# Second layer of a two-layer decoder trunk: weights' pieces in one line with conversions four places behind their loads, the sink's column copied by ScalarE, second values fetched piece by piece, output stores on SyncE

## The chip, the core and the metric

The kernel runs on one core of a Trainium2 chip. The metric is the device time of one execution in microseconds. A core has five engines with instruction queues of their own: TensorE (PE) multiplies matrices into PSUM; VectorE (DVE), ScalarE (ACT) and GpSimd (POOL) do elementwise work; SyncE (SP) here issues most of the DMAs. An engine works through its queue in order: an instruction that has to wait holds up all that stand behind it. ACT can issue DMAs as well.

## What is computed

```python
# layer 1: multi-scale retention; layer 2: sliding-window attention. Both: x + gated branch @ w_out
def swa_layer(x, g_norm, w_in, q_gain, k_gain, sinks, w_out, k_buf=None, v_buf=None):
    h = rmsnorm(x, g_norm)
    proj = h @ w_in
    q, k, v, gate = jnp.split(proj, [SWA_Q, SWA_Q + SWA_KV, SWA_Q + 2 * SWA_KV], axis=-1)
    q = rmsnorm(q.reshape(B, L, SWA_KV_HEADS, SWA_GROUP, SWA_HD), q_gain)
    k = rmsnorm(k.reshape(B, L, SWA_KV_HEADS, SWA_HD), k_gain)
    ...
    scores = jnp.einsum('bnqkgd,bnskd->bnkgqs', qb, kk) * (SWA_HD ** -0.5)
    scores = jnp.where(valid, scores - alibi_slopes() * dist, NEG)
    p = softmax(concatenate([scores, sink_col], -1))[..., :-1]
    o = jnp.einsum('bnkgqs,bnskd->bnqkgd', p, vv)
    ...
    o = o * jax.nn.silu(gate)
    return x + o @ w_out, new_k, new_v
```

There are 1024 prompt tokens in one sequence and 8 single tokens of decode batches with a cache of 128 keys and values each. The model width is 1024. Layer 2 has 16 query heads of 64 in two groups (g = 0, 1) that share a key and a value head, and a window of 128. All is float32; the kernel splits each matmul operand into a rounded high part and the rest, and does three matmuls per product (high x high, high x low, low x high).

## The kernel before, in words

The change lies in layer 2, whose steps are these.

**Weights.** A slot is a block of 1024 x 256 of a weight matrix, `wh` (high) and `wl` (low), three slots in a ring. It is filled in four pieces of 256 KB: SP loads `wr` (L1642, a ring of three), ACT rounds it to `wh` (L1648), POOL subtracts to get `wl` (L1649). There are twelve slots: four for queries, four for gates, four for the output matrix. `job()` is called at fixed places in the program; each call takes a step or a few of the foremost slot's list: three loads at once, nothing in the two calls that end with the marks, then the first conversion, the fourth load and the second conversion, then a conversion per call. `ready` runs the rest of a list at once if a product needs the slot.

**Keys and values** (`kv_mm`, `kv_ev`, `kv_vs`, `kv_v4`). Nine products, for 8 chunks of 128 tokens and the decode tokens, alternate between two PSUM pools, `pj` and `sc`. The values are stored to memory (`vscr2`) and fetched from there in another order as `V4` (L1824), four DMAs for each half; those of group 1 are fetched when group 0 is done, eight DMAs at one place.

**Attention.** A unit ("duo") is one chunk of 128 tokens with four heads (head pair pp = 0 to 3), 32 units in all, one to each step m of a loop that has four steps more at its end. In a step, PE does the scores (`att_s`, L2053), DVE adds the bias (`att_e`, L2069; before it a copy of the sink's column, L2065), takes the maximum (L2074), ACT does four exponentials (`att_p`, L2080), DVE a reciprocal, POOL the normalisation (L2085), DVE a transposition (L2090 and L2093). For the first chunk (c = 0) POOL fills a part of the scores with a constant (L2073) before the maximum. For odd pp PE multiplies with the values two steps later (`att_o`, L2111), and DVE applies the gate (`att_out`). Between these parts stand five calls `fill(src, W)`, which lay about 1 us of projection matmuls each (L1698 to L1700) into PE's queue: first the tiles of queries and gates, then those of the output. A tile goes into one of two `pj` buffers; ACT evicts queries (L1915, L1916), DVE and ACT gates (L1930, L1935, L1941). `decode(m, s)` puts the decode tokens' steps in between, by a table.

**Output** (`so_all`, `so_y`). 24 tiles (ft, ti) of 128 features and a token group ti: 384 tokens for ti = 0, 1 and 264 (256 and the 8 decode tokens) for ti = 2. For each: the residual is loaded (`xr`, L2321, for ti = 2 also L2323; two buffers), 24 matmuls, an add on DVE (L2334), a transposition on DVE (L2263) into `yo`, and four stores (L2266); for ti = 2, one tile later, a transposition on PE, an eviction on ACT (L2272) and a small store (L2273) as well. While attention runs, the four stores are issued by SP, after it by ACT. The small store is on ACT's queue throughout. The last two tiles go another way (L2281).

PE's order is the order of the program, which the scheduler does not alter; the same holds for the other engines in layer 2.

Of the kernel before, what the change touches and what calls it, by code (L numbers as in the profile page):

```python
# [67 lines left out]
def _trunk(ctx, tc, nc, a):  # L68
# [1559 lines left out]
    jobs = []  # L1628

    def wslot(src, turn=True):  # L1630

        slot, box = [], {}

        def first():
# [10 lines left out]
        def conv(i):  # L1645
            js = slice(2 * i, 2 * i + 2)
            raw = box[i]
            nc.scalar.activation(box["hi"][:, js, :], raw, AF.Copy)  # L1648
            nc.gpsimd.tensor_tensor(box["lo"][:, js, :], raw, box["hi"].bitcast(F32)[:, js, :], ALU.subtract)  # L1649
# [4 lines left out]
        slot.append(box)  # L1654
        return slot

    def steps_of(slot, n):
        todo = slot[-1]["todo"]
        for _ in range(n):
            x = todo.pop(0)  # L1660
            while x is None:
                x = todo.pop(0)
            x[0](*x[1:])

    def job():
        while jobs:
            if not jobs[0]["todo"]:
                jobs.pop(0)
                continue
            x = jobs[0]["todo"].pop(0)  # L1670
            if x is None:
                return
            x[0](*x[1:])
            if x[0].__name__ == "conv" and (not jobs[0]["todo"] or jobs[0]["todo"][0][0].__name__ == "conv"):
                return

    def ready(slot):
        box = slot[-1]
        while box["todo"]:
            job()  # L1680
        return slot

    soon = []
# [43 lines left out]
    def w_col(kind, pp):  # L1727
        return wslot(w_in_swa[:, (0 if kind == "q" else 1280) + 256 * pp:(0 if kind == "q" else 1280) + 256 * pp + 256])

    slots = {("q", 0): w_col("q", 0)}  # L1730
    steps_of(slots["q", 0], 4)
# [90 lines left out]
    def kv_v4(h, g=0):  # L1822
        for b in range(4):
            nc.sync.dma_start(out=V4[32 * b:32 * b + 32, 16 * h:16 * h + 16, :],  # L1824
                              in_=vscr2[512 * h:512 * h + 512, 64 * g:64 * g + 64].rearrange("(k i) f -> i k f", i=32))
# [82 lines left out]
    def group_proj(gr):  # L1908
# [16 lines left out]
        def g_ev(pp, pl, ti, ps):  # L1925
# [14 lines left out]
            def rest():  # L1940
                nc.vector.scalar_tensor_tensor(gt, gt, 1.0, gv, ALU.add, ALU.mult)  # L1941
                if ti == 2:
                    nc.vector.scalar_tensor_tensor(gd, gd, 1.0, gxd, ALU.add, ALU.mult)
                    nc.vector.tensor_scalar(gd, gd, 0.5, None, ALU.mult)
# [56 lines left out]
    def ms_ev(xy, pp, ti, sq):  # L2001
# [56 lines left out]

    def att_e(u, xy):
        pp, c = u.pp, u.c  # L2060
        rq = RQ[pp, u.ti]
        st = u.st = atp.tile([128, 4, 161], F32, name="s", bufs=2)
        mx = atp.tile([128, 4], F32, name="mx", bufs=3)
        sm = u.sm = atp.tile([128, 4], F32, name="sm", bufs=3)
        nc.vector.tensor_copy(st[:, :, 160], snk[:, 4 * pp:4 * pp + 4])  # L2065
# [34 lines left out]
    def att_o(u):  # L2100
# [12 lines left out]
        if u.c == 7 and u.g == 0:  # L2113
            later_v4.append(1)

    later_v4 = []
# [112 lines left out]
    def dec_out():  # L2229
        nc.vector.tensor_tensor(god, god, gdec2, ALU.mult)  # L2230
# [26 lines left out]
    def so_y(ft, ti, yt):  # L2257
# [3 lines left out]
        if (ft, ti) not in LAST:  # L2261
            yo = atp.tile([128, 384], F32, tag="qs", name="yo", bufs=6)
            nc.vector.transpose(yo[:, :npr], yt[:, :npr])  # L2263
            for q in range(4):
                f0 = ft * 128 + 32 * q
                (nc.sync if attn[0] else nc.scalar).dma_start(  # L2266
                    out=y_p[0, t0:t0 + npr, f0:f0 + 32].rearrange("(b r) c -> r b c", r=32),
                    in_=yo[32 * q:32 * q + 32, :npr].rearrange("r (b c) -> r b c", c=32))
            if ti == 2:
# [3 lines left out]
                nc.scalar.dma_start(out=y_s[:, 0, ft * 128:ft * 128 + 128], in_=yo[:8, 256:384])  # L2273
# [100 lines left out]
    for n in range(9):  # L2374
# [21 lines left out]
        if 1 <= n <= 4:  # L2396
            steps_of(slots["q", 0], 2 if n == 1 else 1)
        if n == 2:
            slots["q", 1] = w_col("q", 1)
            steps_of(slots["q", 1], 1)  # L2400
            slots["g", 0] = w_col("g", 0)
            steps_of(slots["g", 0], 1)
            jobs.pop()
            jobs.append(slots["q", 1][-1])
        if 2 <= n <= 4:
            steps_of(slots["g", 0], 1)
        if n == 7:
            kv_v4(0)
        if 5 <= n <= 8:
            steps_of(slots["g", 0], 2 if n == 5 else 1)  # L2410
# [11 lines left out]
    kv_v4(1)  # L2422
# [3 lines left out]
    fill(ps, 2.0)  # L2426
    pt = dec_cache(0)
    dec_cache_ev(0, pt)
    fill(ps, 2.0)
    pt = dec_cache(1)  # L2430
# [8 lines left out]
    pvp = xq_.enter_context(tc.tile_pool(name="pvp", bufs=1, space=PSUM))  # L2439
    fill(ps, 1.0)  # L2440
    xy = xy_tile()
    ms_ev(xy, *msq[0], ms_mm(xy, *msq.pop(0)))
    for _ in range(4):
        fill(ps, 1.08)
        now()
        job()
    now()
    left = [1]

    def both():  # L2450
# [10 lines left out]
             (33, 4): (dec_soft, 5), (34, 0): (dec_soft, 6), (34, 1): (dec_vload,), (34, 3): (dec_pt,), (35, 2): (dec_o,),  # L2461
             (35, 3): (dec_out,)}
# [6 lines left out]
    for m in range(NU + 4):  # L2469
# [26 lines left out]
        decode(m, 0)  # L2496
        for fn, args in pend_m:
# [16 lines left out]
        if later_v4:  # L2514
            later_v4.clear()
            kv_v4(0, 1)
            kv_v4(1, 1)
# [16 lines left out]
        x = u  # L2534
        fill(src, W)
    for b in jobs:
        while b["todo"]:
            job()
# [44 lines left out]
```

## Time and profile before

| | |
|---|---|
| three runs | 1262.64, 1262.62, 1257.4 us; median 1262.62 |
| profiled execution | 1262.77 us, span 1261.0 us |
| busy share of the span | PE 97%, DVE 60%, POOL 55%, ACT 47% |
| mean granted clock of PE | 0.993 |
| layer 2, from 905 to 1261 us | PE 328.85 of 356 us busy |

The page gives the busy time of each engine and the chain that ended last. For layer 2 the views that matter are the order in time of one engine, where a number in brackets is idle time of the engine before that instruction with what ended it; the stretches, which give busy time by engine and the granted clock of PE; and the waits of one engine, summed by what it waited for.

### The profile page before, as it was taken

To read this page: it belongs to the slowest core of one execution; us is meant where nothing else is said; L and a number is where in the kernel's file an instruction comes from. 1 tells how busy PE (TensorE), PEld (TensorE's weight loads), DVE (VectorE), ACT (ScalarE), POOL (GpSimd) and SP (SyncE) were. 2 spreads that over 40 slices of the span, in tenths; PEclk is the share of its full clock that TensorE was granted. 3 is DMA by queue.
4 is the path that set the end of the run, shared out by engine and by line. 5 is a ranking of instruction groups with operands and counts; after the bars stand their busy time and mean duration, and the time that the engine had idled before them with its cause. 6 is when DMAs were issued, how large, how long until landed. Compare 5 with 4: busy or idle time off the path is not lost. (4 is left out here: it accounts for less than half of the span.)

```text
span 1261.0 us, 29403 instructions
## 1 busy us (share of the span) xinstructions
PE 1220.8 (97%) x11304; PEld 1155.4 (92%) x11304; DVE 752.9 (60%) x1462; ACT 587.6 (47%) x1482; POOL 689.5 (55%) x740
## 2 busy tenths in 40 slices
PE   7999999999999999999999999999899997999998
PEld 6999999999999999978889999999889886998997
DVE  6954646665666665367775476675255774678421
ACT  6533445545455555478773234454444443454000
POOL 6654544525549899889773266744544453445010
PEclk9999999999999999999999999999989999999999
DMA  6313866677676875365788964774422355155354
GB/s 220 106 55 119 253 198 213 209 232 224 183 226 176 230 221 156 114 199 175 243 259 194 291 202 152 202 224 117 129 68 75 115 159 114 64 188 165 75 130 86
DMA packets 259882, 213.10 MB, mean 169 GB/s; under 512 B 72681, under 2 KB 230757, under 8 KB 259726
## 3 DMA queue, kind: packets, MB, share of 16 engines
q1 hardware_dynamic: 215376, 178.75, 48.4%
q10 hardware_dynamic: 44366, 32.47, 8.6%
q8 instruction: 89, 1.46, 0.5%
q14 instruction: 51, 0.42, 0.1%
HBM read 139.03 MB, written 73.17 MB: 168 GB/s over the span
## 5 line engine op out<-in xcount | busy, mean ns | idle before, releaser
L334 PE MATMUL b<-xh,woh 128*128 128x258 f32 x784 | 223.2, 285 | 0.0
L336 PE MATMUL b<-xh,wol 128*128 128x258 f32 x784 | 221.8, 283 | 0.3 <-POOL wol L225 0.3
L335 PE MATMUL b<-xl,woh 128*128 128x258 f32 x784 | 221.6, 283 | 0.0
L1698 PE MATMUL pj<-SA,wh 128*128 128x384 f32 (+1 forms) x576 | 192.3, 334 | 13.7 <-ACT qs L1916 9.8
L1700 PE MATMUL pj<-SA,wl 128*128 128x384 f32 (+1 forms) x576 | 186.2, 323 | 0.0
L1699 PE MATMUL pj<-SA,wh 128*128 128x384 f32 (+1 forms) x576 | 185.5, 322 | 0.0
L334 PEld LDWEIGHTS b<-xh,woh 128*128 128x128 f32 x784 | 148.0, 189 | 4.1 <-issue 4.1
L335 PEld LDWEIGHTS b<-xl,woh 128*128 128x128 f32 x784 | 148.7, 190 | 0.0
L336 PEld LDWEIGHTS b<-xh,wol 128*128 128x128 f32 x784 | 148.0, 189 | 0.5 <-POOL wol L225 0.5
L225 POOL TENSOR_TENSOR wol<-raw,woh 128x512 fp32r<-128x512 f32 x51 | 66.8, 1318 | 118.0 <-ACT woh L220 106.8
L1698 PEld LDWEIGHTS pj<-SA,wh 128*128 128x128 f32 x576 | 110.0, 191 | 23.2 <-ACT qs L1916 10.5
L327 PE MATMUL b<-woh,xh 128*128 128x256 f32 x448 | 126.6, 283 | 0.0
L328 PE MATMUL b<-wol,xh 128*128 128x256 f32 x448 | 126.0, 281 | 0.0
L329 PE MATMUL b<-woh,xl 128*128 128x256 f32 x448 | 125.6, 280 | 0.0
L1649 POOL TENSOR_TENSOR wl<-wr,wh 128x512 fp32r<-128x512 f32 x48 | 61.6, 1298 | 92.0 <-ACT wh L1648 88.6
L1699 PEld LDWEIGHTS pj<-SA,wh 128*128 128x128 f32 x576 | 110.4, 192 | 0.0
L1700 PEld LDWEIGHTS pj<-SA,wl 128*128 128x128 f32 x576 | 109.9, 191 | 0.0
L327 PEld LDWEIGHTS b<-woh,xh 128*128 128x128 f32 x448 | 84.3, 188 | 5.0 <-issue 2.9
L329 PEld LDWEIGHTS b<-woh,xl 128*128 128x128 f32 x448 | 84.3, 188 | 0.0
L328 PEld LDWEIGHTS b<-wol,xh 128*128 128x128 f32 x448 | 84.3, 188 | 0.0
L220 ACT ACTIVATE woh<-s 128x512 fp32r<-128x512 f32 x88 | 54.1, 623 | 60.1 <-POOL s L210 22.4
L225 DVE TENSOR_TENSOR wol<-s,woh 128x512 fp32r<-128x512 f32 x88 | 67.4, 769 | 20.0 <-ACT woh L220 19.7
(515 smaller groups left out, 3158.4 us busy)
## 6 DMA issues: line engine op xcount, KB each, us to landing
raw<-in_w_in_ret_dram ACTq DMA_DIRECT2D x44, 512.0 KB
st<-in_state_ret_dram SPq DMA_DIRECT2D x64, 256.0 KB
out_dram<-st SPq DMA_DIRECT2D x64, 256.0 KB
vb<-vscr SPq DMA_DIRECT2D x64, 128.0 KB
evp<-qks SPq DMA_DIRECT2D x32, 256.0 KB
evx<-vsc SPq DMA_DIRECT2D x32, 256.0 KB
wr<-in_w_in_swa_dram SPq DMA_DIRECT2D x32, 256.0 KB
pbs<-pb SPq DMA_DIRECT2D x16, 320.0 KB
```

Source lines behind the costliest of these rows:

```text
L220: act(s.op[name, sub][0], src_of(s, name, sub), AF.Copy)
L225: eng.tensor_tensor(lo, src_of(s, name, sub), hi.bitcast(F32), SUB)
L327: mm(dst, xh, wh, start=a and i == 0, stop=False, skip_group_check=True)
L328: mm(dst, xh, wl, start=False, stop=False, skip_group_check=True)
L329: mm(dst, xl, wh, start=False, stop=z, skip_group_check=True)
L334: mm(dst, wh, xh, start=a, stop=False, **sg)
L335: mm(dst, wh, xl, start=False, stop=False, **sg)
L336: mm(dst, wl, xh, start=False, stop=z, **sg)
L1649: nc.gpsimd.tensor_tensor(box["lo"][:, js, :], raw, box["hi"].bitcast(F32)[:, js, :], ALU.subtract)
L1698: mm(ps, hi[:, k, fs], xh[:, k, t0:t1], start=first and k == ks[0], stop=False)
L1699: mm(ps, hi[:, k, fs], xl[:, k, t0:t1], start=False, stop=False)
L1700: mm(ps, lo[:, k, fs], xh[:, k, t0:t1], start=False, stop=last and k == ks[-1])
```

## The change

The list of steps per slot becomes one line of pieces for all slots. At most three pieces are loaded and not yet converted. Each `job()` loads as many as that allows, and converts the oldest if it was loaded at least four calls ago; there is one more call in each step of the loop (five instead of four), and some in the stretch before it. `job` also issues one of the eight fetches of second values, which stand in a list. The sink's column is written by ACT (`att_k`), for the next unit at the end of a step. The factor 0.5 of the decode gate moves into a later product. The copy of `ms` goes from DVE to ACT. Keys and values swap their PSUM pools, so that the ninth product sits in `sc`. The first query slot's loads and conversions keep their places; the second query slot's loads stand ahead of the second value fetches. Three decode steps come one or two places later. The stores of `so_y` are always issued by SP, also the small one.

```diff
-        box["todo"] = [(first,), (load, 0), (load, 1), (load, 2), None, None, (conv, 0), (load, 3)] + [
-            (conv, i) for i in range(1, 4)]
-        jobs.append(box)
...
+    def job(lag=4):
+        tick[0] += 1
+        while pieces and len(flight) < 3:
+            box, i = pieces.pop(0)
+            if "hi" not in box:
+                box["alloc"]()
+            box["load"](i)
+            flight.append((box, i, tick[0]))
+        if flight and flight[0][2] <= tick[0] - lag:
+            box, i, _ = flight.pop(0)
+            box["conv"](i)
+        if later_v4:
+            kv_v4(*later_v4.pop(0))
...
-            kvst[c] = (pjp.tile([128, 512], F32, tag="pj", name="pj") if c % 2 == 0 else
+            kvst[c] = (pjp.tile([128, 512], F32, tag="pj", name="pj") if c % 2 else
...
-                    nc.vector.tensor_scalar(gd, gd, 0.5, None, ALU.mult)
...
-            nc.vector.tensor_copy(ms.rearrange("p (l j r) -> p l j r", l=2, j=2),
-                                  xy[0:1, :, 448:464].rearrange("p j (l r) -> p l j r", l=2))
+            nc.scalar.activation(ms.rearrange("p (l j r) -> p l j r", l=2, j=2),
+                                 xy[0:1, :, 448:464].rearrange("p j (l r) -> p l j r", l=2), AF.Copy)
...
+    def att_k(u):
+        u.st = atp.tile([128, 4, 161], F32, name="s", bufs=2)
+        nc.scalar.activation(u.st[:, :, 160], snk[:, 4 * u.pp:4 * u.pp + 4], AF.Copy)
...
-        nc.vector.tensor_copy(st[:, :, 160], snk[:, 4 * pp:4 * pp + 4])
...
-            later_v4.append(1)
+            later_v4.extend((b_, h, 1) for h in range(2) for b_ in range(4))
...
-        nc.vector.tensor_tensor(god, god, gdec2, ALU.mult)
+        nc.vector.scalar_tensor_tensor(god, god, 0.5, gdec2, ALU.mult, ALU.mult)
...
-                (nc.sync if attn[0] else nc.scalar).dma_start(
+                nc.sync.dma_start(
...
-                nc.scalar.dma_start(out=y_s[:, 0, ft * 128:ft * 128 + 128], in_=yo[:8, 256:384])
+                nc.sync.dma_start(out=y_s[:, 0, ft * 128:ft * 128 + 128], in_=yo[:8, 256:384])
...
-             (33, 4): (dec_soft, 5), (34, 0): (dec_soft, 6), (34, 1): (dec_vload,), (34, 3): (dec_pt,), (35, 2): (dec_o,),
-             (35, 3): (dec_out,)}
+             (33, 4): (dec_soft, 5), (34, 0): (dec_soft, 6), (34, 1): (dec_vload,), (35, 0): (dec_pt,), (35, 3): (dec_o,),
+             (35, 4): (dec_out,)}
...
         decode(m, 0)
+        job()
...
-        if later_v4:
-            later_v4.clear()
-            kv_v4(0, 1)
-            kv_v4(1, 1)
...
+        if m + 1 < NU:
+            att_k(duos[m + 1])
```

What this does to SP's queue is seen best at two places. The first is step m = 17, where group 0 is done. `V` are the value fetches, `wr` the weight loads, `pbs` and `oscr` stores that wait for DVE. SP's rows before:

```order
L2091 DMA pbs<-pb 128x640
L2141 DMA oscr_h<-oh 128x4x128
L2142 DMA oscr_l<-ol 128x4x128
L1824 DMA V_11385<-vscr_75 32x16x64 x8
L1642 DMA wr<-in_w_in_swa_dram 128x2x256 x3
L2010 DMA ms_11366<-ms 4x1x8
L1642 DMA wr<-in_w_in_swa_dram 128x2x256
```

And after:

```order
L1821 DMA V_11385<-vscr_75 32x16x64 x2
L2090 DMA pbs<-pb 128x640
L2138 DMA oscr_h<-oh 128x4x128
L2139 DMA oscr_l<-ol 128x4x128
L1821 DMA V_11385<-vscr_75 32x16x64
L1643 DMA wr<-in_w_in_swa_dram 128x2x256 x3
L1821 DMA V_11385<-vscr_75 32x16x64 x3
L2006 DMA ms_11366<-ms 4x1x8
L1821 DMA V_11385<-vscr_75 32x16x64
L2090 DMA pbs<-pb 128x640
```

The eight fetches no longer stand in one block ahead of the three loads; three stand ahead of them, and five behind.

The second place is the output, after the end of attention. `xr` are the residuals' loads, `yo` the stores. SP's rows before, from tile (1,1)'s load to tile (4,1)'s:

```order
L2321 DMA xr_15961<-xscr 128x384
L2321 DMA xr_16007<-xscr 128x384
L2321 DMA xr_16042<-xscr 128x384
L2321 DMA xr_16077<-xscr 128x256
L2323 DMA xr_16077<-xdec 128x8
L2321 DMA xr_16107<-xscr 128x256
L2323 DMA xr_16107<-xdec 128x8
L1642 DMA wr<-in_w_out_swa_dram 128x2x256 x3
L2321 DMA xr_16155<-xscr 128x384
```

And after, from tile (3,1)'s load to the small store of tile (1,2):

```order
L2318 DMA xr_16034<-xscr 128x384
L2263 DMA out_dram<-yo 32x12x32 x4
L2318 DMA xr_16069<-xscr 128x256
L2320 DMA xr_16069<-xdec 128x8
L2318 DMA xr_16099<-xscr 128x256
L2320 DMA xr_16099<-xdec 128x8
L1643 DMA wr<-in_w_out_swa_dram 128x2x256 x3
L2263 DMA out_dram<-yo 32x8x32 x4
L2270 DMA out_dram<-yo 8x128
L2318 DMA xr_16147<-xscr 128x384
L2263 DMA out_dram<-yo 32x8x32 x4
L2270 DMA out_dram<-yo 8x128
```

Before, only loads stood there; now each group of four stores, and the small stores, stand between the load of one tile and that of a later one.

More of the change, by code (lines that the diff above doesn't have):

```diff
@@ L1626, in _trunk, with wslot, alloc @@
     wp = ctx.enter_context(tc.tile_pool(name="wp", bufs=1, reuse_waits="tile"))
[L1628 to L1634, printed above, removed]
+    pieces, flight, tick = [], [], [0]
+    def wslot(src, turn=True, auto=True):
+        box = dict(n=0)
+        slot = [box]
+        def alloc():
             box["hi"] = wp.tile([128, 8, 256], F32R, tag="wh", bufs=3, name="wh")
@@ L1649, in conv @@
             nc.gpsimd.tensor_tensor(box["lo"][:, js, :], raw, box["hi"].bitcast(F32)[:, js, :], ALU.subtract)
-        box["todo"] = [(first,), (load, 0), (load, 1), (load, 2), None, None, (conv, 0), (load, 3)] + [
-            (conv, i) for i in range(1, 4)]
-        jobs.append(box)
-        slot.append(box)
-        return slot
[L1657 to L1675, printed above, removed]
+            box["n"] += 1
+        box.update(alloc=alloc, load=load, conv=conv)
+        if auto:
+            pieces.extend((box, i) for i in range(4))
+        return slot
+    def job(lag=4):
[11 more added lines that the diff above has]
+            kv_v4(*later_v4.pop(0))
     def ready(slot):
-        box = slot[-1]
-        while box["todo"]:
-            job()
+        while slot[-1]["n"] < 4:
+            job(0)
         return slot
-    soon = []
+    soon, later_v4 = [], []
     def now():
@@ L1725, in io, with w_col @@
         return iop2.tile([128, 384], dt, tag=tag, bufs=bufs, name=tag)
[L1727 to L1731, printed above, removed]
+    def w_col(kind, pp, auto=True):
+        c0 = (0 if kind == "q" else 1280) + 256 * pp
+        return wslot(w_in_swa[:, c0:c0 + 256], True, auto)
+    slots = {("q", 0): w_col("q", 0, False)}
+    wq0 = slots["q", 0][-1]
+    wq0["alloc"]()
+    for j in range(3):
+        wq0["load"](j)
     iop2 = ctx.enter_context(tc.tile_pool(name="iop2", bufs=1))
@@ L2061, in att_e @@
         rq = RQ[pp, u.ti]
[L2062 removed]
+        st = u.st
         mx = atp.tile([128, 4], F32, name="mx", bufs=3)
         sm = u.sm = atp.tile([128, 4], F32, name="sm", bufs=3)
[L2065 removed]
         for pl in range(2):
@@ L2396, in _trunk @@
         if 1 <= n <= 4:
-            steps_of(slots["q", 0], 2 if n == 1 else 1)
+            wq0["conv"](n - 1)
+        if n == 1:
+            wq0["load"](3)
         if n == 2:
[L2399 to L2404, printed above, removed]
+            slots["q", 1] = w_col("q", 1, False)
+            slots["q", 1][-1]["alloc"]()
+            slots["g", 0] = w_col("g", 0, False)
+            wg0 = slots["g", 0][-1]
+            wg0["alloc"]()
         if 2 <= n <= 4:
-            steps_of(slots["g", 0], 1)
+            wg0["load"](n - 2)
         if n == 7:
-            kv_v4(0)
+            for b in range(4):
+                kv_v4(b, 0, 0)
         if 5 <= n <= 8:
-            steps_of(slots["g", 0], 2 if n == 5 else 1)
+            wg0["conv"](n - 5)
+        if n == 5:
+            wg0["load"](3)
     sg_.close()
@@ L2421, in _trunk @@
     kv_tr(7)
-    kv_v4(1)
+    pieces.extend((slots["q", 1][-1], i) for i in range(4))
+    job()
+    for b in range(4):
+        kv_v4(b, 1, 0)
     kv_out()
@@ L2534, in _trunk @@
         x = u
+        if m + 1 < NU:
+            att_k(duos[m + 1])
         fill(src, W)
-    for b in jobs:
-        while b["todo"]:
-            job()
+    while pieces or flight:
+        job(0)
     xq_.close()
```

15 lines of the change are left out of this document (9 added, 6 removed).

## The prediction

> **What bounds the kernel now.** I read the page first, then the stretches of 20 us, the order in time of TensorE (PE) with its idle times, the waits of ScalarE (ACT), and last the chain that ended last.
>
> ```profile
> span 1261.0 us, 29403 instructions
> PE 1220.8 (97%) x11304; PEld 1155.4 (92%) x11304; DVE 752.9 (60%) x1462; ACT 587.6 (47%) x1482; POOL 689.5 (55%) x740
> ```
>
> The run took 1262.77 us, 1.8 more than its span and 0.15 above the median of 1262.62. PE is busy for 97% of it, so no part can give much except where PE stands idle or runs slowly. The change touches only layer 2, from about 860 us on. There the idle times of PE and the granted clock are few and easy to find:
>
> ```profile
> 900.00:920.00 20.00, 15.51 (x199) 13.95 (x188) 3.67 (x14) 8.42 (x21) 9.98 (x10) 0.86 0.22 79
> 920.00:940.00 20.00, 20.00 (x225) 18.98 (x232) 13.20 (x34) 8.12 (x27) 11.69 (x8) 0.97 0.28 87
> ...
> 1040.00:1060.00 20.00, 15.78 (x282) 14.96 (x283) 10.94 (x31) 8.39 (x29) 8.77 (x10) 0.91 0.42 90
> 1060.00:1080.00 20.00, 15.66 (x176) 13.56 (x175) 9.33 (x22) 9.30 (x33) 8.64 (x8) 0.91 0.45 116
> ...
> 1180.00:1200.00 20.00, 18.57 (x106) 17.54 (x104) 5.83 (x12) 1.04 (x5) 0.00 (x0) 0.91 0.43 96
> ```
>
> ```profile
> 915.24 0.59 PE L1698 MATMUL pj<-SA,wh 128*128 128x264 f32 x1 [4.49 <-ACT qs L1916]
> ...
> 983.37 1.09 PE L2111 MATMUL o<-R,V 32*64 32x128 f32 x40 [1.95 <-DVE R L2093]
> ...
> 1032.58 1.42 PE L2111 MATMUL o<-R,V 32*64 32x128 f32 x80 [0.97 <-issue]
> ...
> 1044.22 0.59 PE L1698 MATMUL pj<-SA,wh 128*128 128x264 f32 x1 [4.80 <-ACT qs L1916]
> ...
> 1069.94 0.44 PE L1698 MATMUL pj<-SA,wh 128*128 128x384 f32 x1 [3.62 <-DVE sq L1930]
> ...
> 1182.53 0.67 PE L104 MATMUL xy<-ident,rbc 16*128 16x16 f32 x9 [1.37 <-DVE rbc L2196]
> ```
>
> The second column of a stretch is PE's busy time, the third last the granted clock. Each long idle time costs twice: 4.49 us of waiting at 915, then (0.14 + 0.03) x 20 = 3.4 us of clock; 4.80 at 1044 and 3.62 at 1070, each with 0.09 x 20 = 1.8 us of clock. What they wait for is an ACT that stands still itself:
>
> ```profile
> ACT wh L1648 <- DMA wr<-in_w_in_swa_dram: 29.3, 11, 6.2
> ```
>
> In eleven places ACT waits in its conversion of a weight piece for that piece to land, 29.3 us in all, and the PSUM evictions behind it wait too. From 1160 us on something else ends last. The chain that ended last is a loop over output tiles, no longer PE:
>
> ```profile
> 1167.44 0.57 DVE sq L2334
> ...
> 1187.65 0.57 DVE sq L2334
> 1188.24 0.59 DVE yo L2263
> 1188.85 0.33 SPq L2266
> ...
> 1190.78 2.52 DMA xr<-xscr
> 1193.39 0.57 DVE sq L2334
> ...
> 1199.48 0.57 DVE sq L2334
> ```
>
> The residual is added to a tile (sq), VectorE (DVE) transposes it (yo), SyncE (SP) issues its four stores, and only then the load of the next tile's residual (xr), for which the next add waits. One turn takes 1193.39 - 1187.65 = 5.74 us; the five turns from 1167.44 to 1199.48 took 6.41 on average. PE runs two tiles ahead, all that its two buffers allow; at 1200 it has to wait for an add, so the lead is used up:
>
> ```profile
> 1200.10 0.44 PE L1698 MATMUL pj<-SA,wh 128*128 128x384 f32 x1 [0.16 <-DVE sq L2334]
> ```
>
> **The change part by part.**
>
> *Weights' pieces in one line.* A conversion now stands four places behind its load, in PE's program some 5 us instead of 2. The three long idle times, one by one. At 915 two things were late: ACT's conversions, and the memory fill of the first unit's scores on GpSimd (POOL), queued behind three conversions:
>
> ```profile
> 906.22 1.26 DVE L2069 SCALAR_TENSOR_TENSOR s<-xy,rq,ndp 128x160 f32<-128x160 f32 x4 [4.71 <-PE xy L2053]
> 907.01 3.79 POOL L1649 TENSOR_TENSOR wl<-wr,wh 128x512 fp32r<-128x512 f32 x3 [3.20 <-DMA wr<-in_w_in_swa_dram]
> 910.74 1.55 POOL L2073 MEMSET s<- 32x512 f32 x4
> 912.32 0.82 DVE L2074 TENSOR_REDUCE mx<-s 128x4 f32<-128x644 f32 x1 [4.84 <-POOL s L2073]
> ...
> 914.62 0.56 ACT L1916 ACTIVATE qs<-pj,gq 128x384 f32<-128x384 f32 x1
> ```
>
> The new order loads this slot ahead of the value fetches and cache copies and converts earlier, so the fill can start when DVE is done at 907.48. Then fill 1.55, maximum 0.82, and from its end to the eviction's end 915.18 - 913.14 = 2.04: done at 911.9. PE stood from 910.75, so 1.15 us of the wait stays, hidden by nothing. Saved: 3.3 us, and the 3.4 of clock if so short a wait brings none: 6.7. At 1044 the same fill (the unit is again the first of its head pair) keeps about as much: 4.80 - 1.15 + 1.8 = 5.4. At 1070 ACT waited for this:
>
> ```profile
> 1054.28 6.26 SPq L1824 DMA_DIRECT2D V<-vscr  x8
> ...
> 1065.80 1.26 ACT L1648 ACTIVATE wh<-wr 128x512 fp32r<-128x512 f32 x2 [6.20 <-DMA wr<-in_w_in_swa_dram]
> ```
>
> Eight fetches of second values held SP for 6.26 us ahead of the loads of the next slot. They are now issued one at each place and the loads after three of them; the fetched values are first used some eight units later. Saved: 3.62 + 1.8 = 5.4. The 1.95 at 983 has the same cause (DVE behind a tanh that stood behind a conversion) and goes; the 0.97 at 1032 goes with DVE's relief, below. Sum: 6.7 + 5.4 + 5.4 + 1.95 + 0.97 = 20.4. What is late next, wherever PE comes earlier, is the chain scores, maximum, exponentials, normalisation of each unit, and loads that stand behind SP's waits for DVE. I take 18 us; the ends are 10 (the third long wait goes whole, a third of the rest) and 24 (the two waits of 1.15 go too, and small ones not listed).
>
> *Sink's column on ACT, one product less on DVE.*
>
> ```profile
> L2065 DVE COPY s<-snk 128x4 f32<-128x4 f32 x32 | 11.2, 349 | 0.0
> ...
> L1944 DVE TENSOR_SCALAR gdec<-gdec 128x8 f32<-128x8 f32 x8 | 3.6, 448 | 0.3
> ```
>
> ```profile
> 1134.84 0.19 ACT L1938 ACTIVATE gdec<-sq 128x8 f32<-128x8 f32 x1
> ```
>
> DVE loses 14.8 us of busy time; PE waits for DVE in few places, all counted above. The nearest row for the copy on ACT is 0.19 us, so 32 of them take 6 us of an engine that is busy 47%. The copy waits for the buffer that DVE frees one unit earlier; behind it stand the next evictions, but ACT had to wait for that same DVE to get here. Nothing, with 1 us to each side.
>
> *Swap of PSUM pools for keys and values, later decode steps.* PE has no idle time in the key stage but one of a microsecond at its start, so plus or minus 1. The 1.37 at 1182 goes with the later step, but PE is ahead of the adds there: nothing.
>
> *Stores on SP.* With the stores on ACT, the last 16 adds went about at PE's pace. In the new order each load of a residual stands behind the stores of the tile before, to the end, so the turn of the chain applies to all of them. The rows that it needs:
>
> ```profile
> 1205.20 0.32 SPq L2321 DMA_DIRECT2D xr<-xscr  x1
> ...
> 1207.55 0.43 DVE L2334 TENSOR_TENSOR sq<-pj,xr 128x264 f32<-128x264 f32 x1 [1.76 <-DMA xr<-xdec]
> ...
> 1252.95 0.56 DVE L2334 TENSOR_TENSOR sq<-pj,xr 128x384 f32<-128x384 f32 x1 [2.94 <-PE pj L1700]
> 1255.88 0.43 DVE L2334 TENSOR_TENSOR sq<-pj,xr 128x264 f32<-128x264 f32 x1 [2.38 <-PE pj L1700]
> ```
>
> ```profile
> 1239.44 1.94 ACTq L2266 DMA_DIRECT2D out_dram<-yo  x4
> 1241.73 0.29 ACTq L2273 DMA_DIRECT2D out_dram<-yo  x1
> ```
>
> From add to load is 1190.78 - 1187.65 = 3.13 us; a load of 384 columns then takes 2.6 to its add, one of 264 takes 1207.55 - 1205.20 = 2.35. From the add of tile (1,1) at 1199.48 to the last, the new order has: two plain turns, 11.5; three that end in a narrow tile, 3.13 + 2.35 = 5.5 each, 16.4; four behind a narrow tile's stores (add and transposition 0.9, four stores 1.9, small store 0.3, load 2.35 or 2.6) 5.5 to 5.75 each, 22.5; three behind two tiles' stores (2 x 1.9 + 0.3 + load 2.6 + add and transposition 1.1), 7.8 each, 23.3; four adds whose load follows at once, 0.9 each, 3.5. Together 77.2. Before it was 1255.88 - 1199.48 = 56.4. The cost is 20.8 us. Its cover would be PE's lead, and that is spent by 1200. With 5.4 us in a quiet turn it is 17, with the 6.41 of the busy turns 29.
>
> **Sum:** 1262.8 - 18 + 20.8 = 1265.6 us.
>
> [...] A narrow tile's 24 matmuls take PE 1255.88 - 1252.95 = 2.9 us, a wide one's 384/264 of that, 4.3; so in turns of 5.5 to 5.8 us PE will wait 1.5 to 2.6. The row at 1182.53 shows that 1.37 us came with a stretch at 0.91. [...]
>
> **The rivals.** *The loop on SP stays hidden.* If residuals land in time after all, the tail goes at PE's pace, and the 1.71 us at
>
> ```profile
> 1232.67 0.27 PE L104 MATMUL tr<-ident,sq 128*8 128x128 f32 x1 [1.71 <-ACT yo L2272]
> ```
>
> go too, since ACT no longer stands in store issues: 1262.8 - 18 - 1.7 = 1243.1. For it speaks that two residual buffers exist; against it that SP's new order has no place where a load overtakes the stores, and that this loop is seen between 1167 and 1199. *The gains don't come.* If the fill on POOL and the loads behind SP's waits keep PE standing as long as a late conversion did, with 8 us gained, it is 1262.8 - 8 + 20.8 = 1275.6, slower; it decides from under 14.5 us of gain (1269). *The clock falls in the tail.*
>
> ```profile
> 1200.00:1261.00 61.00, 54.88 (x373) 53.84 (x373) 14.59 (x32) 5.31 (x14) 5.08 (x4) 0.98 0.51 105
> ```
>
> PE has 54.9 us of work there. If each of some twelve waits costs 1.8 us of clock, that is 76.5, still under 77.2; if 3.4, as at 915, it is 95.7 and PE is last again: 18.5 more, 1284.
>
> **How the numbers follow.** 0.5%, about 6.3 us, is what a measurement of this kernel can tell from no change: 1256.3 to 1268.9. Forecast 0.62, of which 0.44 falls within that, 0.13 above, 0.05 below. Loop hidden 0.12, faster. Gains missing 0.20, of which 0.04 within. Clock 0.06, slower. So faster 0.17, same 0.48, slower 0.35. The range, 1254 to 1279, takes in the ends of gain (24 with a cost of 17: 1255.8) and of cost (18 with 29: 1273.8; 8 with 24: 1278.8), and leaves out the hidden loop and the clock.
>
> **What would show it.** Right: ACT's waits for wr fall from 29.3 us to a few; no PE idle time over 2 us between 900 and 1150; the first add of an output tile comes about 18 us earlier; from then on every add waits for xr, at 5.5 to 6.4 us a turn and near 7.8 behind two tiles' stores, with PE idle in each. Wrong: adds in the tail that wait for PE (then 1243), a long PE wait still at the first unit of a head pair (then 1276), or a clock well under 0.9 after 1180.

## The result and the profile after

The changed kernel takes 1267.18 us (median, 1265.94 to 1270.85), the kernel before, beside it on the same chip, 1261.15 us (1257.4 to 1262.64). The ratio is 1.0055, with a 95% interval from 1.0034 to 1.0076: half a per cent more. The forecast was 1265.6 in a range from 1254 to 1279.

Behind the small difference stand two large ones. The first rows are the head of the page after; then come ACT's waits, then PE's order in time in layer 2, where the brackets hold the idle time ahead of an instruction and what ended it.

```profile
span 1264.1 us, 29412 instructions
PE 1223.8 (97%) x11304; PEld 1158.3 (92%) x11304; DVE 737.5 (58%) x1418; ACT 590.8 (47%) x1518; POOL 690.6 (55%) x740
```

```profile
ACT wh L1649 <- DMA wr<-in_w_in_swa_dram: 8.5, 5, 4.0
```

```profile
908.69 0.39 PE L1692 MATMUL pj<-SA,wh 128*128 128x264 f32 x1 [1.37 <-ACT qs L1913]
...
1028.29 0.39 PE L1692 MATMUL pj<-SA,wh 128*128 128x264 f32 x1 [2.10 <-ACT qs L1913]
...
1189.22 0.39 PE L1692 MATMUL pj<-SA,wh 128*128 128x264 f32 x1 [2.63 <-DVE sq L2331]
...
1210.35 0.59 PE L1692 MATMUL pj<-SA,wh 128*128 128x264 f32 x1 [3.71 <-DVE sq L2331]
...
1242.45 0.69 PE L1692 MATMUL pj<-SA,wh 128*128 128x384 f32 x1 [4.54 <-DVE sq L2331]
```

ACT's waits for weight pieces fell from 29.3 us to 8.5, and of PE's long waits before the output two short ones are left. In their place PE now waits in the output, for adds on DVE. What the adds wait for is seen in their own rows, from tile (1,1) to the end:

```profile
1177.05 0.56 DVE L2331 TENSOR_TENSOR sq<-pj,xr 128x384 f32<-128x384 f32 x1 [4.10 <-DMA xr<-xscr]
1182.78 0.56 DVE L2331 TENSOR_TENSOR sq<-pj,xr 128x384 f32<-128x384 f32 x1 [4.56 <-DMA xr<-xscr]
...
1201.88 0.56 DVE L2331 TENSOR_TENSOR sq<-pj,xr 128x384 f32<-128x384 f32 x1 [5.76 <-DMA xr<-xscr]
1209.74 0.56 DVE L2331 TENSOR_TENSOR sq<-pj,xr 128x384 f32<-128x384 f32 x1 [6.49 <-DMA xr<-xscr]
...
1234.11 0.56 DVE L2331 TENSOR_TENSOR sq<-pj,xr 128x384 f32<-128x384 f32 x1 [4.78 <-DMA xr<-xscr]
1241.84 0.56 DVE L2331 TENSOR_TENSOR sq<-pj,xr 128x384 f32<-128x384 f32 x1 [6.36 <-DMA xr<-xscr]
...
1249.39 0.56 DVE L2331 TENSOR_TENSOR sq<-pj,xr 128x384 f32<-128x384 f32 x1 [1.11 <-PE pj L1694]
1257.85 1.03 DVE L2331 TENSOR_TENSOR sq<-pj,xr 128x384 f32<-128x384 f32 x2 [7.08 <-DMA xr<-xscr]
```

`x2` in the last row stands for two adds, one right behind the other. All of the adds shown but one (at 1249.39) wait for the residual xr, from 1201.88 to 1241.84 for 4.8 to 6.5 us. A plain turn takes 5.73 us (1177.05 to 1182.78), a turn behind two tiles' stores 7.73 to 8.46 (1201.88 to 1209.74, 1234.11 to 1241.84, 1249.39 to 1257.85).

Four marks split each trace of this study: the first matmul of layer 2 (keys and values), the first add of an output tile, the add of tile (1,1), which is the eighth, and the last add. The start of layer 2 lies at 857.9 in the trace before and between 853.9 and 859.5 in the others, although layer 1 is the same in all kernels; so the stretches inside layer 2 compare better than the totals. The median is over all executions of a kernel, the ratio is to the kernel before as it was measured beside each, and the stretches are from the execution that was profiled. All in us:

| kernel | median | ratio to before, 95% interval | start of layer 2 to first add | first add to (1,1) | (1,1) to last add |
|---|---|---|---|---|---|
| before | 1261.15 | | 294.6 | 47.0 | 56.4 |
| after | 1267.18 | 1.0055 (1.0034 to 1.0076) | 273.7 | 48.7 | 81.4 |
| before_stores_on_sp | 1282.81 | 1.0164 (1.0146 to 1.0182) | 292.9 | 45.9 | 82.0 |
| stores_on_act | 1244.39 | 0.9852 (0.9819 to 0.9886) | 272.2 | 48.8 | 58.6 |
| residual_ahead | 1234.38 | 0.9787 (0.9761 to 0.9813) | 273.5 | 41.5 | 57.8 |
| ahead_and_act | 1235.59 | 0.9795 (0.9773 to 0.9817) | 272.4 | 44.7 | 57.8 |
| lag_2 | 1270.11 | 1.0067 (1.0043 to 1.009) | 281.5 | 45.3 | 81.1 |
| values_in_one_block | 1265.14 | 1.0044 (1.0028 to 1.0061) | 272.2 | 49.2 | 80.6 |
| lag_2_and_block | 1268.67 | 1.006 (1.0045 to 1.0075) | 278.5 | 44.7 | 80.6 |
| block_old_place | 1269.9 | 1.0079 (1.0053 to 1.0106) | 275.4 | 49.0 | 80.9 |
| column_on_dve | 1268.15 | 1.0064 (1.0041 to 1.0088) | 275.1 | 48.8 | 81.4 |
| no_fill | 1234.83 | 0.9787 (0.9766 to 0.9807) | 270.3 | 44.5 | 57.8 |
| ahead_decode_early | 1239.39 | 0.9829 (0.9813 to 0.9846) | 272.6 | 47.7 | 57.8 |
| ahead_and_block | 1239.35 | 0.9824 (0.9798 to 0.985) | 273.1 | 43.4 | 57.8 |

For the change itself: layer 2 began 3.3 us earlier (1.05 of that is a wait of PE at its start that is gone, the rest the spread of layer 1), the first add came 20.8 us sooner after it, the stretch to (1,1) took 1.7 more, the tail 25.0 more, the end 0.5 more (from the last add to the end of the span, 5.6 against 5.1). -3.3 - 20.8 + 1.7 + 25.0 + 0.5 = +3.1, the difference of the two spans. The 20.8 us are 14.9 less of idle PE (18.6 before, 3.6 after) and nearly all of the rest is clock: by the stretches of 20 us, 7.0 us were lost before and 1.8 after.

### The profile page after: what moved, and what is told of

Read it like the earlier page. It is cut to its first block, busy times and chain, and to the rows that moved or that the text cites. A ratio compares the mean times of both kernels' runs of the same rounds, so it can differ in the third digit from the quotient of the medians.

```text
span 1264.1 us, 29412 instructions
## 1 busy us (share of the span) xinstructions
PE 1223.8 (97%) x11304; PEld 1158.3 (92%) x11304; DVE 737.5 (58%) x1418; ACT 590.8 (47%) x1518; POOL 690.6 (55%) x740
## 4 chain that ended last, share of the span: by engine, by line
PE 80%; DMA 5%; DVE 5%; SPq 3%; POOL 3%; issue 2%; ACT 1%; ACTq 0%; DVEq 0%; POOLq 0%
PE S L1317 9%; PE b L334 8%; PE b L336 8%; PE b L335 8%; PE pj L1692 5%; PE pj L1694 5%; PE pj L1693 5%; PE b L327 4%; PE b L328 4%; PE b L329 4%; SPq L2263 3%; DMA xr<-xscr 2%; PE xy L2049 2%; PE tr L104 2%; PE b L543 2%
```

## The experiments

**The stores back on ACT** (`stores_on_act`): the changed kernel, its other parts untouched.

```diff
-                nc.sync.dma_start(
+                (nc.sync if attn[0] else nc.scalar).dma_start(
...
-                nc.sync.dma_start(out=y_s[:, 0, ft * 128:ft * 128 + 128], in_=yo[:8, 256:384])
+                nc.scalar.dma_start(out=y_s[:, 0, ft * 128:ft * 128 + 128], in_=yo[:8, 256:384])
```

> The kernel after, with the stores after attention back on ScalarE as in the kernel before; the rest of the change stays. Theory (the residual loads' place behind the stores in SyncE's queue costs the time): the first output add stays near 1128 us, the 16 adds after tile (1,1) take about 56 us instead of 81, the whole about 1241 us, 1.6% under the kernel before. Rival (the tail is long for another reason: the later decode steps, conversions in the tail, or a clock that idle times have lowered): the tail stays over 70 us and the whole at 1258 to 1267 us.

It took 1244.39 us, and the tail 58.6. The adds now wait for PE, 40.5 us in all; of the 14.2 for xr, 12.5 lie ahead of tile (1,1), where SP still issues the stores:

```profile
L2331 DVE TENSOR_TENSOR sq<-pj,xr 128x384 f32<-128x384 f32 (+1 forms) x24 | 12.4, 515 | 59.7 <-PE pj L1694 40.5 <-DMA xr<-xscr 14.2 <-DMA out_dram<-yo 5.0
```

In the changed kernel the group of these adds (its idle time behind the second bar, with what ended most of it) waits for PE for 1.8 us in all:

```profile
L2331 DVE TENSOR_TENSOR sq<-pj,xr 128x384 f32<-128x384 f32 (+1 forms) x24 | 12.4, 515 | 80.9 <-DMA xr<-xscr 53.4 <-DMA xr<-xdec 25.1 <-PE pj L1694 1.8
```

So the place of the stores costs the whole gain of 20.8 us, and more: 81.4 - 58.6 = 22.8 us.

**Only the stores, on the kernel before** (`before_stores_on_sp`): the same lines, changed the other way.

```diff
-                (nc.sync if attn[0] else nc.scalar).dma_start(
+                nc.sync.dma_start(
...
-                nc.scalar.dma_start(out=y_s[:, 0, ft * 128:ft * 128 + 128], in_=yo[:8, 256:384])
+                nc.sync.dma_start(out=y_s[:, 0, ft * 128:ft * 128 + 128], in_=yo[:8, 256:384])
```

> The kernel before with this one part of the change: all of these stores issued by SyncE. Theory: nothing moves before 1199 us, then the 16 adds take 77 to 82 us instead of 56, so 1261 + 21 to 25 = 1282 to 1286 us. Rival (the cost belongs to another part): 1261 to 1266 us.

It took 1282.81 us, with the tail at 82.0 and the adds waiting as in the changed kernel:

```profile
DVE sq L2334 <- DMA xr<-xscr: 52.6, 12, 7.0
...
DVE sq L2334 <- DMA xr<-xdec: 25.0, 6, 6.0
```

The cost is the same without the other parts: 25.6 us more in the tail than before.

**The load ahead of the stores** (`residual_ahead`): all stores stay on SP, but a residual is asked for as soon as one of the two buffers is free, which puts its load one tile earlier in SP's queue, ahead of the stores that used to hold it up.

```diff
-            pend_x.append((ft, ti))
...
-        pend_x, xrs = [], []
+        pend_x, xrs = list(order), []
```

> The kernel after, all stores on SyncE, but a residual is asked for one tile earlier, so that its load stands ahead of the stores of the tile before. Theory (the place in the queue): PE sets the pace again, the adds wait for PE and not for xr, 1238 to 1243 us. Rival (one queue for stores and loads slows the transfers themselves, or SyncE has too much to issue): the adds still wait for xr, 1255 us or more.

It took 1234.38 us, the lowest median of the study (two other kernels with this edit lie within 1.3 us of it). Nothing but the place of the loads in the queue is changed, and the waits for residuals are gone but for 5.4 us:

```profile
L2330 DVE TENSOR_TENSOR sq<-pj,xr 128x384 f32<-128x384 f32 (+1 forms) x24 | 12.3, 512 | 46.3 <-PE pj L1694 40.8 <-DMA xr<-xdec 5.4
```

The tail is at 57.8, as short as with the stores on ACT. The total is below the 1238 to 1243 expected, by what came from the stretch ahead of the tail, from 48.7 to 41.5. The loop of add, stores and load bound the last output tiles of that stretch too: the last three adds waited 4.1 to 4.4 us each for xr in the changed kernel, 3.8 to 4.6 in the kernel before, and none of the three waits for xr now. A part of the 7.2 us is clock, since the changed kernel lost (0.09 + 0.09) x 20 = 3.6 us there and this one none (1.00 in both stretches):

```profile
1140.00:1160.00 20.00, 19.41 (x191) 18.19 (x192) 13.03 (x21) 2.52 (x4) 1.12 (x1) 0.91 0.41 97
1160.00:1180.00 20.00, 19.02 (x109) 18.04 (x108) 5.11 (x11) 1.04 (x5) 0.00 (x0) 0.91 0.43 91
```

As all stores are still on SP, neither their number nor their sharing a queue with the loads costs time that this run shows.

**Both cures** (`ahead_and_act`): the edits of `stores_on_act` and `residual_ahead` together.

```diff
+                (nc.sync if attn[0] else nc.scalar).dma_start(
...
+        pend_x, xrs = list(order), []
```

> Both cures at once: residuals asked for a tile earlier and the stores after attention on ScalarE. Theory: they cure the same wait, so together no more than 2 us under the better of the two, about 1240 us. Rival (queue place and issue load are two costs): 5 us or more under the better one.

It took 1235.59 us, with the tail at 57.8 again: in the tail it is one wait, and either cure takes it whole. The stretch ahead of it took 44.7, with 0.92 and 0.91 of the clock from 1140 to 1180, so about 4 us of the 7.2 remain where the clock falls as in the changed kernel.

**Two places instead of four** (`lag_2`), the first of the runs on where the 20.8 us came from.

```diff
-    def job(lag=4):
+    def job(lag=2):
```

> The changed kernel with each conversion of a weight piece two places behind its load in place of four; nothing else differs. My theory: the distance between load and conversion is what made most of the 20 us before the output, so ScalarE's waits for wr, 8.5 us in the changed kernel and 29.3 in the kernel before, come back to 20 to 30, PE gets waits of several us at the first projections again, the first add of an output tile comes 5 to 12 us later, and the time is 1272 to 1279 (from 1267). Rival: the order of the loads (in one line, ahead of the value fetches) and the spread fetches made it, not the distance; then the waits for wr stay under 12 us and the time within 3 us of 1267.

The mechanism is there: ACT's waits are back, PE's wait at the second head pair is up from 2.10 to 3.14 us, others of 1 us come back, and the first add is 7.8 us later.

```profile
ACT wh L1649 <- DMA wr<-in_w_in_swa_dram: 26.1, 10, 7.3
```

```profile
911.34 0.39 PE L1692 MATMUL pj<-SA,wh 128*128 128x264 f32 x1 [1.47 <-ACT qs L1913]
...
983.32 1.42 PE L2110 MATMUL o<-R,V 32*64 32x128 f32 x80 [1.02 <-issue]
...
1033.96 0.59 PE L1692 MATMUL pj<-SA,wh 128*128 128x264 f32 x1 [3.14 <-ACT qs L1913]
```

The time, 1270.11, is only 3 us over that of the changed kernel, short of the 1272 to 1279 expected: the stretch from the first add to (1,1) took 45.3 instead of 48.7. Of these 3.4 us, 1.2 are a shorter wait of PE ahead of the product of the decoded queries (0.38 instead of 1.60), and the clock from 1140 to 1160, 1.00 instead of 0.91, makes 1.8. Of the 7.8 us at the first add, 1.6 are clock too: 0.83 here from 1020 to 1040, 0.91 in the changed kernel.

**Second values at one place** (`values_in_one_block`).

```diff
-        if later_v4:
+        while later_v4:
```

> The changed kernel with the eight fetches of second values issued at one place again; the weights' order stays. My theory: the eight fetches hold SP for 6.3 us ahead of the next loads, so the wait of 3.6 us that the kernel before had at 1070 comes back with some of its 1.8 us of clock, the first add comes 3.6 to 5.4 us later and the time is 1271 to 1273. Rival: with conversions four places behind the loads the block is covered; no PE wait over 1 us between 1040 and 1080, and the time stays within 2 us of 1267.

1265.14 us, the first add at 272.2, and no PE wait of 0.5 us or more came back between 1040 and 1080. My theory fell, the rival held. That the first add comes 1.5 us sooner than in the changed kernel is no merit of the block: the clock from 1020 to 1040 is 1.00 here and 0.91 there, which is 1.8 us.

**Both undone** (`lag_2_and_block`): the edits of the last two together.

```diff
-    def job(lag=4):
+    def job(lag=2):
...
-        if later_v4:
+        while later_v4:
```

> The changed kernel with the conversions two places behind the loads and the eight fetches of second values at one place, both undone together; the one line of weight pieces stays. Each alone left the wait at 1070 away. My theory now: either cures that wait, since four places are enough to hide a block of fetches of 6.3 us, so with both undone a PE wait of 2 to 4 us between 1055 and 1080 is back, ScalarE's longest wait for wr is 6 us or more there, and the first add of an output tile comes 3 to 6 us later than with two places alone (281.5 us from the first matmul of layer 2); the time is 1272 to 1276. Rival: the order of the pieces in one line cured that wait, since loads that are due now stand ahead of the block: no PE wait over 1 us there and the time within 2 us of the 1270.1 with two places alone.

1268.67 us, the first add at 278.5, and again no PE wait of 0.3 us or more between 1040 and 1080. That falls too: it isn't that either part alone cures the wait at 1070. SP's order shows why. In this kernel the block of eight stands here:

```profile
1032.85 6.60 SPq L1821 DMA_DIRECT2D V<-vscr  x8
1041.67 0.34 SPq L2090 DMA_DIRECT2D pbs<-pb  x1
1042.11 0.39 SPq L2138 DMA_DIRECT2D oscr_h<-oh  x1
1042.59 0.53 SPq L2139 DMA_DIRECT2D oscr_l<-ol  x1
1043.21 2.24 SPq L1643 DMA_DIRECT2D wr<-in_w_in_swa_dram  x3
```

It lies in a stretch in which SP has nothing else to do, ahead of three stores. In the kernel before it stood behind those three stores, straight ahead of the loads. These two experiments had undone the pieces, but not the place. The first add here comes 6.3 us later than in `values_in_one_block`; that is what two places instead of four cost, with 1.8 us of clock in it (0.91 here and 1.00 there from 1020 to 1040).

**The block at its old place** (`block_old_place`), with the four places kept.

```diff
-        if later_v4:
-            kv_v4(*later_v4.pop(0))
...
             reloads()
+        while later_v4:
+            kv_v4(*later_v4.pop(0))
```

> The changed kernel with the eight fetches of second values in one block at the very place of the kernel before on SP: behind the value products' next score store and the next two output stores, straight ahead of three loads of weights. In the two runs with a block so far it stood ahead of those three stores, some 10 us earlier, in a stretch in which no load was due. My theory now: that earlier place cured the wait at 1070, not the pieces and not the distance alone; with the old place ScalarE waits 4 us or more for wr near 1050 to 1060, a PE wait of 1 to 3 us is back between 1045 and 1080, the first add comes 275 to 278 us after the first matmul of layer 2 (273.7 in the changed kernel), and the time is 1268 to 1272. Rival: four places between load and conversion cover the block at any place; no PE wait over 0.5 us between 1045 and 1080, first add at 272 to 274, time within 2 us of 1267.

1269.9 us, the first add at 275.4, and the waits are back, as the theory has it:

```profile
1048.41 0.63 ACT L1649 ACTIVATE wh<-wr 128x512 fp32r<-128x512 f32 x1 [5.26 <-DMA wr<-in_w_in_swa_dram]
```

```profile
1050.57 0.44 PE L1690 MATMUL pj<-SA,wh 128*128 128x384 f32 x1 [1.61 <-DVE sq L1925]
1059.60 0.40 PE L1985 MATMUL xy<-sq,ones 64*32 64x96 f32 x16 [0.92 <-ACT sq L1910]
```

The earlier place of the fetches is what counts. This kernel differs from `values_in_one_block` in that place alone, the block being issued from 1037.01 instead of 1028.85, and the clock from 1020 to 1040 is 1.00 in both:

```profile
1020.00:1040.00 20.00, 17.90 (x409) 16.54 (x409) 10.04 (x25) 11.46 (x37) 13.65 (x13) 1.00 0.80 186
```

```profile
1020.00:1040.00 20.00, 17.91 (x382) 16.54 (x370) 10.63 (x27) 10.76 (x36) 13.67 (x13) 1.00 0.49 138
```

The first add is 275.4 - 272.2 = 3.2 us later. Against the changed kernel it is only 1.7, mostly because that one lost 1.8 us of clock there. At the earlier place, whether the fetches come one by one or in a block makes no difference that these runs show; pieces at the old place were not run.

**The column on DVE** (`column_on_dve`).

```diff
-        nc.scalar.activation(u.st[:, :, 160], snk[:, 4 * u.pp:4 * u.pp + 4], AF.Copy)
...
+        nc.vector.tensor_copy(st[:, :, 160], snk[:, 4 * pp:4 * pp + 4])
...
+                    nc.vector.tensor_scalar(gd, gd, 0.5, None, ALU.mult)
...
-        nc.vector.scalar_tensor_tensor(god, god, 0.5, gdec2, ALU.mult, ALU.mult)
+        nc.vector.tensor_tensor(god, god, gdec2, ALU.mult)
```

> The changed kernel with the sink's column copied by VectorE again at its old place, and the product by one half of the last gates back on VectorE. My theory: VectorE's 14.8 us of busy time were beside PE's work; the small wait of 0.97 us before the value products may come back, the time is 1267 to 1269. Rival: these small copies stood behind GpSimd's work and in the chain of each unit (scores, maximum, exponentials), so that their removal made a good part of the gain: the time is 1271 or more, with VectorE's waits before the score rows longer and the first add 4 us or more later.

1268.15 us, the first add at 275.1, 1.4 us later. The small wait ahead of the value products did not come back; instead the wait at the first unit of the second head pair grew from 2.10 to 3.57:

```profile
1034.53 0.39 PE L1692 MATMUL pj<-SA,wh 128*128 128x264 f32 x1 [3.57 <-ACT qs L1913]
```

**Without the fill** (`no_fill`), on `residual_ahead`.

```diff
-        if c == 0:
-            for b in range(4):
-                nc.gpsimd.memset(st[32 * b:32 * b + 32, :, 0:128 - 32 * b], NEG)
```

> The kernel with the residual asked for one tile earlier (1234.4), in which GpSimd's memory fill of the masked part of each head pair's first unit is left out, so that these scores stay unmasked. My theory: the two waits of PE that are left at the first projections, 1.37 and 2.10 us, come from this fill in the chain from scores to maximum, and the second brings a stretch at 0.91 of the clock: they go or fall under 0.5 us, and the time falls by 3 to 5 us to 1229 to 1231. Rival: the chain is as late for another reason (VectorE's order, exponentials, the eviction on ScalarE), the waits stay above 1 us and the time within 1.5 us of 1234.

1234.83 us: no gain, as the rival has it, but for other reasons. The second wait, 2.10 us, is gone with its slow stretch, and the first add comes 3.2 us sooner. The first wait stays, at 1.32:

```profile
905.36 0.63 ACT L1649 ACTIVATE wh<-wr 128x512 fp32r<-128x512 f32 x1 [3.97 <-DMA wr<-in_w_in_swa_dram]
906.01 1.28 ACT L2076 ACT_TABLE_LOAD   x1
...
909.13 0.39 PE L1692 MATMUL pj<-SA,wh 128*128 128x264 f32 x1 [1.32 <-ACT qs L1913]
```

There the fill was not what ended last: a fourth piece that lands late holds ACT for 3.97 us, then it loads a function table, 1.28 us, and only then come the exponentials, with the eviction `qs` behind them. And the 3.2 us that were gained at the first add are lost again behind it, in the clock:

```profile
1120.00:1140.00 20.00, 18.36 (x287) 16.26 (x286) 14.78 (x28) 9.33 (x29) 14.98 (x11) 0.94 0.72 204
1140.00:1160.00 20.00, 20.00 (x190) 18.65 (x188) 13.22 (x21) 2.17 (x4) 0.00 (x0) 0.97 0.35 71
1160.00:1180.00 20.00, 20.00 (x116) 19.63 (x116) 5.24 (x12) 0.76 (x4) 0.00 (x0) 0.91 0.45 95
```

(0.06 + 0.03 + 0.09) x 20 = 3.6 us of clock, where `residual_ahead` has 1.00 in all three. Why the clock fell there in the one and not in the other isn't settled; both have a PE wait ahead of the decoded queries' product, 1.64 here, 1.32 there.

**Decoding at its old places** (`ahead_decode_early`), on `residual_ahead`.

```diff
-(34, 1): (dec_vload,), (35, 0): (dec_pt,), (35, 3): (dec_o,),
-             (35, 4): (dec_out,)}
+(34, 1): (dec_vload,), (34, 3): (dec_pt,), (35, 2): (dec_o,),
+             (35, 3): (dec_out,)}
```

> The kernel with the residual asked for one tile earlier (1234.4), with the last three steps of decoding at the places of the kernel before. The later places are followed by a PE wait of 1.3 to 1.6 us ahead of the product of decoded queries in every run of the new order, which the kernel before has not. My theory: that wait comes with the later places, so it goes, and with it what half-clock stretch it starts; the gain is 1 to 3 us, to 1231 to 1233. Rival: the places are free, PE is ahead of the adds there or the wait moves to the next step; the time is within 1 us of 1234.4.

1239.39 us, 5 more; theory and rival both fall. The wait did not go, it grew from 1.32 to 2.1, and two came with the old places:

```profile
PE o L2166 <- DVE ot L2118: 2.1, 1, 2.1
PE xy L2219 <- DMA vc<-in_cache_swa_v_dram: 0.7, 1, 0.7
PE xy L104 <- DVE rbc L2193: 0.4, 1, 0.4
```

The expectation has the wait at 1.3 to 1.6 us in every run of the new order; it was 0.38 in `lag_2` and 1.77 in `column_on_dve`. At the later places PE had no wait for the cached values (`vc`) in `residual_ahead`, and one of 0.45 us in `lag_2_and_block`. The stretch from the first add to (1,1) is 6.2 us longer. The three waits make 1.9 us more than the one of `residual_ahead`; the larger part is clock again, 0.98, 0.94 and 0.83 from 1120 to 1180, (0.02 + 0.06 + 0.17) x 20 = 5.0 us. That the waits brought this loss is not shown by a run of its own, but the mean clock was 0.995 to 0.997 in all four executions of this kernel, and 0.998 or 0.999 in those of `residual_ahead`.

**The block, on `residual_ahead`** (`ahead_and_block`): the edits of `residual_ahead` and `values_in_one_block` together.

```diff
-        if later_v4:
+        while later_v4:
```

> The kernel with the residual asked for one tile earlier, and the second values fetched at one place. In the changed kernel the block made the time no longer (1265.1 against 1267.2). My theory: the spread of these fetches is worth nothing once the conversions stand four places behind, so the time is 1233 to 1235.5. Rival: the block was hidden in the changed kernel by the later wait for residuals; without that wait it costs 2 us or more, to 1236.5 or above.

Inconclusive: 1239.35 us, but the single times reach from 1233.81 to 1241.61. They go with the mean granted clock of their executions: 1233.81 at 1.000, 1239.48 at 0.997, 1239.22 at 0.996, 1241.61 at 0.995. In the trace layer 2 began 3.1 us later, and the stretch behind the first add took 1.9 more, of which 1.8 is clock (0.91 from 1160 to 1180, where `residual_ahead` has 1.00). The first add came at 273.1 instead of 273.5, but ahead of it only `residual_ahead` lost 1.8 us of clock. So the runs can't tell a cost of the block of up to some 1.4 us from none; the total alone would fit the rival's 1236.5 or above, but no 2 us of cost are seen in the trace.

## Why the prediction was right, and where not

**The two terms and their signs** were right. Forecast: 18 us gained ahead of the output, 20.8 lost in the tail, both from rows of the trace before. Measured: 20.8 and 25.0. That the total came within 1.6 us of the forecast is in part luck: the errors, 2.8 us more gain and 4.2 more cost, nearly cancel, and so do the three parts that were not forecast, a start of layer 2 that is 3.3 us earlier, 1.7 more up to tile (1,1) and 0.5 more at the end.

**The gain** was put at 20.4 by its list and taken as 18; it was 20.8. ACT's waits for wr fell "to a few": 8.5. Place by place, wait and clock together, the list brought 6.5 at 915 (6.7 forecast), 2.7 at 1044 (5.4), 5.4 at 1070 (5.4) and 2.9 at the two small waits (2.9), 17.5 in all; most of the other 3.3 are five waits of 0.3 to 0.95 us that the list did not have, 2.6 us, all gone. The list's causes held only in part. For 915, "1.15 us of the wait stays", for the fill: 1.37 stayed, for a late piece and a table load instead (`no_fill`). For 1044, 1.15 and no loss of clock were forecast: 2.10 stayed, for the fill, and with 1.8 us of clock. Rows of POOL in the changed kernel show the fill still behind a subtraction, 1.2 us after DVE had finished the scores (at 1021.59 + 1.26 = 1022.85):

```profile
1022.77 1.30 POOL L1650 TENSOR_TENSOR wl<-wr,wh 128x512 fp32r<-128x512 f32 x1
1024.01 1.55 POOL L2072 MEMSET s<- 32x512 f32 x4
```

For 1070 the cause was right, the cure half so: the earlier place does it, without the pieces. The 0.97 at 1032 does not hang on DVE's relief, to which the forecast put it: with the relief undone (`column_on_dve`) it did not come back. "Nothing, with 1 us to each side" for DVE's relief was 1.4. Taken apart, the distance of four places makes 6.3 to 7.8 us of the gain (lag_2_and_block against values_in_one_block, lag_2 against after; 4.5 to 6.2 without the clock), the place of the fetches 3.2, the column 1.4. If these add up, which no run shows, some 8 to 10 us are left that were not separated: the line of pieces, and the additional call in each step.

**The tail** was 4.2 us too short. Its mechanism, load behind stores behind an add, is shown by four runs. By the classes of the forecast, from the rows above and those left out there: plain turns 11.55 us (11.5 forecast); turns behind two tiles' stores 24.05 (23.3); adds that follow at once 4.1 (3.5); the other seven 41.7 (38.9). The other seven hold most of the error, and among them two turns of 6.55 us instead of 5.5 to 5.75. The chain that ended last shows what was missed in one of them, one of four stores of a tile that took a microsecond longer to issue:

```profile
1196.14 0.35 SPq L2263
1196.54 0.44 SPq L2263
1197.04 0.45 SPq L2263
1197.52 1.48 SPq L2263
1199.10 0.30 SPq L2270
1199.45 2.34 DMA xr<-xscr
```

What held this issue for 1.48 us isn't seen in the trace; it happened once more, at 1218.15 with 1.57. Both belong to the first stores after the loads of two narrow tiles had been issued together; whether that is the reason is not shown.

**The rivals.** The hidden loop was wrong for this change, since every load stands behind stores, as the forecast said; with a load ahead of them it would have been right, at 1234.38. The missing gains were wrong: 20.8 us came. The sum has no clock in it for the waits of the tail; that was the author's estimate, and no run shows that such waits leave the clock as it is. The clock did fall in the tail, to 0.91 in two stretches of 20 us from 1180 and to 0.83 in the last, with waits of 0.5 to 4.5 us; but nearly all of the adds waited for residuals all the while, so it cost next to nothing. The exception is the add at 1249.39, which waited 1.11 us for PE, whose clock was 0.50 to 0.54 from 1242 to 1248: it came 1.54 us behind the add before it, where two others that follow at once came 0.98 and 1.00 behind, so some 0.5 us.

**The signs.** Those for being right came, with two exceptions: PE's idle time at 1028 was 2.10 us, just over the 2 named, and in the tail not every add waits for xr, nor does PE stand idle in every turn. Of the signs of being wrong, a clock well under 0.9 after 1180 did come (0.83 from 1240 to 1260), without the time of 1284 that the forecast tied to it.

**Seen, but not weighed:** the forecast found the loop between 1167 and 1199 in the kernel before, and reckoned only with its spreading to the tail. That it could be removed there too was not asked; with the load ahead, the stretch from the first add to (1,1) went from 48.7 us to 41.5, and to 44.7 where the clock fell as in the changed kernel.

## What to carry to other kernels

Here a queue that issued both the stores of one result and the load of the next operand made a loop, in which the load waited for the arithmetic that the stores waited for, 5.73 us a plain turn. Cure it by asking for the load a buffer earlier, ahead of the stores, if a buffer is free for it; here the one edit was worth some 33 us (1267.18 to 1234.38), more than either large term of the change. Stores on another queue cured the tail as well (58.6 us instead of 81.4), but were tried only behind the end of attention. When a change moves the time little, look for two large terms of opposite sign before calling its parts idle, and when part of it is undone in a test, compare the order of the queues, not the source lines: an undone edit can still leave the instructions at their new place. And before a microsecond or two is put down to an edit, compare the granted clock of the stretches: here 1.8 us of it hid nearly half of what the fetches' old place cost.

## What the runs showed of the hardware

In these runs the length of the wait alone did not set the clock's loss behind it. From 1020 to 1040 PE stood idle for 2.1 us both in `residual_ahead` (20 - 17.91) and in `ahead_decode_early` (20 - 17.90); the clock was 0.91 in the one and 1.00 in the other. These are their rows, in that order, the clock third from the end.

```profile
1020.00:1040.00 20.00, 17.91 (x349) 16.45 (x335) 9.82 (x24) 10.34 (x35) 13.53 (x13) 0.91 0.48 132
```

```profile
1020.00:1040.00 20.00, 17.90 (x358) 16.54 (x344) 11.03 (x27) 10.36 (x35) 13.55 (x13) 1.00 0.55 150
```

In the kernel before, too, the wait of 1.37 us at 1182 was followed by a clock of 0.51 from 1184 to 1186, that of 1.95 at 983 by 1.00 from 984 to 988. Seen closer, in the changed kernel, the slow stretch is at half the clock and short:

```profile
1028.00:1030.00 2.00, 1.72 (x40) 1.58 (x48) 0.18 (x1) 2.00 (x8) 0.35 (x1) 0.85 0.65 164
1030.00:1032.00 2.00, 2.00 (x77) 1.59 (x71) 0.31 (x1) 1.34 (x6) 2.00 (x2) 0.50 0.47 106
1032.00:1034.00 2.00, 2.00 (x62) 1.74 (x47) 1.06 (x4) 0.63 (x1) 1.37 (x2) 0.80 0.01 4
```

(0.15 + 0.50 + 0.20) x 2 = 1.7 us are lost, so by this estimate it lasts 3.4 us at one half. The losses of 3.6 and 5.0 us told of above are about two and three of these. What starts such a stretch isn't shown by these runs.

Four stores took 1.86 to 1.88 us to issue on SP in the plain turns of the changed kernel, but the place of the stores ahead of the loads cost 22.8 us in the tail: here the order within the queue counted, not only the time of issuing.
